# Two weight buffers for the block products, and an output projection in halves of 512 columns

## The chip, the cores and the metric

The kernel runs on one core of a Trainium2 chip. The metric is the device time of one execution in microseconds (us), here the median of 3 runs. A profiled execution gives the trace from which all rows below come; its engines are called PE (matrix multiplication, with its weight loads as PEld), DVE (vector), ACT (scalar activations), POOL, and SP, which here only issues DMA transfers.

## The reference

One layer on x of 1024 tokens by 1024 features, in float32. What matters here:

```
h = rmsnorm(x, g_mix)
u, c_g, b_g, q, k, v, sg, m_c, m_r = split(h @ w_in)         # nine blocks of columns
y_conv = (b_g * causal_dwconv(c_g * u, conv_w)) @ w_out_conv   # 3 taps along the tokens
o = rmsnorm(retention(rope(q), rope(k), v), g_ret)
y_ret = (silu(sg) * o) @ w_out_ret
x = x + (sigmoid(m_c) * y_conv + sigmoid(m_r) * y_ret) @ w_o   # the output projection
x = x + hier_moe(rmsnorm(x, g_moe), ...)                       # 32 experts, 2 per token
ple = rmsnorm(p @ w_ple_proj, g_ple_post)
x = x + sigmoid(rmsnorm(x, g_ple_in) @ w_ple_gate) * ple
out = rmsnorm(x, g_final)
```

## The kernel before

Every float32 product is made of three fp32r products (mm3, lines 192 to 195): the operands are split into a high part, which ACT writes (split, L188), and a low part, which DVE writes (L189), and PE adds high by high, high by low and low by high.

The products with w_in for u, c, b, sg, m_c and m_r go in blocks of 256 columns. One block (seven, L409 on) loads 1 MB of weights into a part of the buffer `both` (L411), forms sums of its quarters on DVE (L441 into `bt`, L442 in place in `both`, L443 into `bt`), splits seven pieces `pc`, and PE runs seven partial products of 12 matmuls of 128x512 each, with the token halves in the rotating accumulators sa, sb, sc, sd. Between them ACT (L452) and DVE (L453, L457, L458, and L464 to L467) combine the accumulators; the fourth product into sd may start only when L458 has read sd. The list of blocks has 24 entries: n = 0 to 7 (m_c, m_r) together with the retention, which uses `both[:, 1]` for its chunks; n = 8 to 19 are u, c and b for four groups of columns (conv_pair); n = 20 to 23 are sg. `raw()` gives the place of the block's weights: always `both[:, 0]`. In conv_pair DVE also makes the three taps (L490 to L492) and L497.

After that the mix (y, out_conv and out_ret) and the output projection (out_proj, L558) run for each half of 512 tokens, hf = 0 and 1. out_proj goes by quarters of 256 columns of w_o: 512 KB chunks of weights (`wor`, L199; split into `wos`), two accumulators `oa` and `ob` that hold two token tiles each, then DVE adds x (in `ring`, loaded by L566) and multiplies by the gain of the expert norm; PE turns the result (h2q, h2p, L595), ACT or DVE copies it (h2T), and PE multiplies by the router's weights (lp, L604). x2d and h2d are stores for later stages. In hf = 1 `look(i)` (L734) issues the first expert loads `raw`. Then come the router (lg), the projection of p (ple: pa, stores to pled, L796) and the experts (L908 to L953).

The tiles are allocated from pools and a scheduler fixes the order of each engine's instructions before the run; every engine executes its own list in order. SP has at most eight DMAs outstanding: each issue also waits for the one eight before it.

Of the kernel before, what the change touches and what calls it, by code (L numbers as in the profile page):

```python
# [10 lines left out]
F32 = mybir.dt.float32  # L11
F32R = mybir.dt.float32r
BF = mybir.dt.bfloat16
I32 = mybir.dt.int32
AF = mybir.ActivationFunctionType
OP = mybir.AluOpType
# [4 lines left out]
S, D, NH, DK, DV = 1024, 1024, 8, 64, 128  # L21
# [54 lines left out]
def tile_kernel(ctx, tc, cst, x, p, g_mix, w_in, conv_w, g_ret, w_out_conv, w_out_ret, w_o, g_moe,  # L76
                w_rg, b_rg, w_re, b_re, w_exp_gate, w_exp_up, w_exp_down, g_ple_in, w_ple_gate,
                w_ple_proj, g_ple_post, g_final, out, dbg=None, stop=99):
    nc = tc.nc
    V, A, P, T, Y = nc.vector, nc.scalar, nc.gpsimd, nc.tensor, nc.sync  # L80
    dbg = dbg or {}
    x, p, out = x[0], p[0, 0], out[0]
    w_in, w_o, w_out_conv, w_out_ret = w_in[0], w_o[0], w_out_conv[0], w_out_ret[0]
# [15 lines left out]
    wk = dst.enter_context(tc.tile_pool(name="wk", bufs=2, side="right", reuse_waits="tile"))  # L99
    ps = dst.enter_context(tc.tile_pool(name="ps", bufs=1, space=PSUM, reuse_waits="tile"))  # L100

    def bt(name, dt=F32R):
        return big.tile([128, 4096], dt, name=name, tag="big", bufs=8)

    def w2k(name, dt=F32):
        return wk.tile([128, 512], dt, name=name, tag="w2k", bufs=NW)

    def row2(name, src):
        g = [w2k(name), w2k(name)]
        for i in range(2):  # L110
            Y.dma_start(out=g[i], in_=bass.AP(tensor=src.tensor, offset=src.offset + i * 512, ap=[[0, 128], [1, 512]]))
        return g

    def acc(name):
        return ps.tile([128, 512], F32, name=name, tag="acc", bufs=4)

    def trp(name):
        return ps.tile([128, 4, 128], F32, name=name, tag="tr", bufs=1)
# [6 lines left out]
    wr = xgb[:, 644:1412].rearrange("p (k n) -> p k n", k=8)  # L125
# [20 lines left out]
    ident = cs[:, C_ID:C_ID + 128]  # L146
# [30 lines left out]
    x2d = dram.tile([S, D], F32, name="x2d")  # L177
    h2d = dram.tile([S, D + 1], F32, name="h2d")
# [8 lines left out]
    def split(src, hi, lo):  # L187
        a = A.activation(hi, src, AF.Copy)  # L188
        V.tensor_tensor(lo, src, hi, op=OP.subtract)  # L189
        return a.ins  # L190

    def mm3(o, lh, ll, rh, rl, start, stop, skip=False):
        T.matmul(o, lh, rh, start=start, stop=False, skip_group_check=skip)  # L193
        T.matmul(o, lh, rl, start=False, stop=False, skip_group_check=skip)  # L194
        return T.matmul(o, ll, rh, start=False, stop=stop, skip_group_check=skip).ins  # L195

    def wraw(src, k0, nk, c0, nn, name):
        raw = rawp.tile([128, 1024], F32, name=name + "r", tag="raw", bufs=2)
        Y.dma_start(out=raw.rearrange("p (k n) -> p k n", k=nk),  # L199
                    in_=src[k0 * 128:(k0 + nk) * 128, c0:c0 + nn].rearrange("(k p) n -> p k n", p=128))  # L200
        return raw

    def wchunk(src, k0, nk, c0, nn, name):
        raw = ahead.pop() if ahead else wraw(src, k0, nk, c0, nn, name)
        hl = wp.tile([128, 2, 1024], F32R, name=name + "s", tag="hl", bufs=3)
        with tc.issue_after(started.pop()) if started else nullcontext():
            split(raw, hl[:, 0], hl[:, 1])
        return hl.rearrange("p s (k n) -> p s k n", k=nk)
# [319 lines left out]
    def parts(src, hf, at=None):  # L528
        hi, lo = (bt(n).rearrange("p (f t) -> p f t", f=8) for n in ("ph", "pl"))
        for f in range(0, 8, 2) if at else ():  # L530
            split(at[f // 4][:, f % 4:f % 4 + 2], hi[:, f:f + 2], lo[:, f:f + 2])
        for f in range(8) if not at else ():
            t = w2k("pr")
            Y.dma_start(out=t, in_=src[f * 128:f * 128 + 128, hf * 512:hf * 512 + 512])
            split(t, hi[:, f], lo[:, f])
        return hi, lo
# [19 lines left out]
                then()  # L556

    def out_proj(hf, mhv, mlv, gm):  # L558
        ring = bt("ring", F32).rearrange("p (r t n) -> p r t n", r=4, t=4)
        ss = wk.tile([128, 4, 4], F32, name="x2ss", bufs=2)  # L560
        lp = ps.tile([128, 4, 128], F32, name="lp", tag="kv", bufs=1)
        h2l = shared.rearrange("p (t n) -> p t n", t=4)
        rows = slice(hf * 512, hf * 512 + 512)

        def load(cc):
            Y.dma_start(out=ring[:, cc % 2],  # L566
                        in_=x[rows, cc * 256:cc * 256 + 256].rearrange("(t p) n -> p t n", p=128))

        load(0)
        for cc in range(4):  # L570
            a = [acc("oa"), acc("ob")]
            ck = slice(cc * 256, (cc + 1) * 256)
            x2 = ring[:, cc % 2]
            h2 = ring[:, 2 + cc % 2] if cc < 3 else h2l[:, :, 0:256]
            if cc < 3:
                load(cc + 1)
            for kh in range(2):
                wc = wchunk(w_o, kh * 4, 4, cc * 256, 256, "wo")
                for t in range(4):
                    for k in range(4):  # L580
                        kk = kh * 4 + k
                        mm3(a[t // 2][:, (t % 2) * 256:(t % 2) * 256 + 256],
                            mhv[:, kk, t * 128:(t + 1) * 128], mlv[:, kk, t * 128:(t + 1) * 128],
                            wc[:, 0, k], wc[:, 1, k], kk == 0 and t % 2 == 0, kk == 7, True)
            for b in range(2):
                tt = slice(2 * b, 2 * b + 2)
                V.tensor_tensor(x2[:, tt], a[b].rearrange("p (t n) -> p t n", t=2), x2[:, tt], op=OP.add)
                V.tensor_tensor(h2[:, tt], x2[:, tt], gm[cc // 2][:, None, (cc % 2) * 256:(cc % 2) * 256 + 256].to_broadcast([128, 2, 256]), op=OP.mult)
                for t in (2 * b, 2 * b + 1):
                    j = w2k("x2j", BF)[:, 0:256]  # L590
                    A.activation(j, x2[:, t], AF.Square, accum_out=ss[:, t, cc:cc + 1])
                pt = trp("h2p") if b else ps.tile([128, 4, 128], F32, name="h2q", tag="S", bufs=1)
                for t in (2 * b, 2 * b + 1):
                    for j in range(2):
                        T.transpose(pt[:, (t % 2) * 2 + j], h2[:, t, j * 128:(j + 1) * 128], ident)  # L595
                hT = w2k("h2T").rearrange("p (a b) -> p a b", a=4)
                if b == 0:
                    A.activation(hT, pt, AF.Copy)
                else:
                    V.tensor_copy(hT, pt)  # L600
                for t in (2 * b, 2 * b + 1):
                    for j in range(2):
                        k = 2 * cc + j
                        T.matmul(lp[:, t, 0:96], hT[:, (t % 2) * 2 + j], wr[:, k],  # L604
                                 start=cc == 0 and t == 0 and j == 0, stop=k == 7, skip_group_check=True)
            Y.dma_start(out=x2d[rows, ck].rearrange("(t p) n -> p t n", p=128), in_=x2)
            if cc < 3:
                Y.dma_start(out=h2d[rows, ck].rearrange("(t p) n -> p t n", p=128), in_=h2)
            if hf == 1 and cc < 2:
                look(cc)  # L610
        return ss, lp, h2l


# [103 lines left out]
    def wview(e, w):  # L717
        src, k = wsrc[w]
        return src[e].rearrange("(p k) n -> p (k n)", k=k)
# [7 lines left out]
    def look(i):  # L727
        for c in order[len(raws):i + 1]:
            raws[c] = bt("raw", F32)
            for h in range(2):  # L730
                late = len(raws) == 8 and h == 1
                sl = slice(h * 2048, h * 2048 + 2048)
                with tc.issue_after(gathers[-1]) if late else nullcontext():
                    (P if late else Y).dma_start(out=raws[c][:, sl], in_=wview(*c)[:, sl])  # L734
# [79 lines left out]
            'S3': (*s34, 0), 'S4': (*s34, 4)}  # L814
    both = bt("both", F32).rearrange("p (r n) -> p r n", r=2)

    def raw():
        return both[:, 0]

    for n in range(8):  # L820
        gate_pair(n // 4, n % 4, raw, left, retention(n, both[:, 1]))
# [15 lines left out]
    z, r = parts(zd, 0, zr), parts(rd, 0)  # L837
    for hf in range(2):
        mhv, mlv = (bt(n).rearrange("p (f t) -> p f t", f=8) for n in ("mh", "ml"))
        mix(hf, z, r, mhv, mlv, (lambda: router(0, *late)) if hf else None)  # L840
        if hf == 0:
            r, z = parts(rd, 1), parts(zd, 1)
        gm = row2("gm", g_moe)
# [403 lines left out]
```

## Time and profile before

| what | value |
|---|---|
| median of 3 runs | 1788.19 us (1787.86 to 1793.71) |
| the profiled execution | 1788.15 us, of which the trace's span is 1786.4 us |
| PE busy | 1720.2 us, 96% of the span |
| DVE, ACT, POOL busy | 1269.6, 903.3, 157.6 us |
| mean granted PE clock | 0.989 |
| moved by DMA | 397.68 MB, mean 223 GB/s |

Times of the trace count from the span's start. "Busy" of PE is modelled: matmuls overlap in the pipeline, so the duration of one is longer than the distance from one start to the next. "Idle before" of a row is the time in which its engine had nothing to run, and the releaser is what ended it.

### The profile page before, as it was taken

How to read it: one execution, taken by the hardware profiler on the slowest of the kernel's cores; microseconds unless marked ns; L12 is line 12 of the kernel's file. 1: busy time of each engine (PE TensorE's matmuls, PEld its weight loads, DVE VectorE, ACT ScalarE, POOL GpSimd, SP SyncE). 2: the span in 40 equal slices, each digit the busy share in tenths (PEclk: the TensorE clock that was granted, in tenths of full speed). 3: DMA queues.
4: the chain of work that ended last, by engine and by line, in shares of the span. 5: the costliest groups of instructions: out<-in, count | busy, mean ns of one | idle time of the engine just before them, and what ended most of it. 6: DMA issues, size and time to landing. Idle time of an engine off the chain costs nothing. (4 is left out here: it accounts for less than half of the span.)

```text
span 1786.4 us, 22831 instructions
## 1 busy us (share of the span) xinstructions
PE 1720.2 (96%) x8447; PEld 1348.9 (76%) x8447; DVE 1269.6 (71%) x1747; ACT 903.3 (51%) x1354; POOL 157.6 (9%) x157
## 2 busy tenths in 40 slices
PE   6999999999999999899999998999999999999697
PEld 5878788888787878788988975676767676666586
DVE  5559576675776776646464467999999988888674
ACT  4343443443222223424322347888888877778542
POOL 1000000000000000000000013121212221100010
PEclk9999999999999999999999999999999999999899
DMA  6534444433113226657666879999999999996561
GB/s 226 155 103 136 153 133 144 137 119 106 63 56 118 71 94 190 189 185 227 166 194 200 272 231 356 365 369 382 378 372 374 369 373 351 368 397 267 202 253 64
DMA packets 174628, 397.68 MB, mean 223 GB/s; under 512 B 14796, under 2 KB 101908, under 8 KB 148916
## 3 DMA queue, kind: packets, MB, share of 16 engines
q1 hardware_dynamic: 165012, 378.19, 61.0%
q0 software_dynamic: 9504, 18.02, 3.3%
q8 instruction: 67, 1.10, 0.3%
q14 instruction: 45, 0.37, 0.1%
HBM read 344.77 MB, written 57.68 MB: 225 GB/s over the span
## 5 line engine op out<-in xcount | busy, mean ns | idle before, releaser
L910 DVE TENSOR_TENSOR hc<-raw,hc 128x1024 fp32r<-128x1024 f32 x128 | 154.3, 1223 | 21.1 <-ACT hc L908 20.0
L910 DVE TENSOR_TENSOR hb<-raw,hb 128x1024 fp32r<-128x1024 f32 x128 | 153.9, 1220 | 15.2 <-ACT hb L908 13.8
L910 DVE TENSOR_TENSOR ha<-raw,ha 128x1024 fp32r<-128x1024 f32 x128 | 154.1, 1222 | 13.7 <-ACT ha L908 11.7
L908 ACT ACTIVATE ha<-raw 128x1024 fp32r<-128x1024 f32 x128 | 132.7, 1058 | 26.6 <-PE y L195 15.3
L908 ACT ACTIVATE hb<-raw 128x1024 fp32r<-128x1024 f32 x128 | 132.8, 1057 | 21.1 <-PE u L195 11.6
L908 ACT ACTIVATE hc<-raw 128x1024 fp32r<-128x1024 f32 x128 | 132.6, 1057 | 17.2 <-PE y L195 5.1
L188 ACT ACTIVATE pc<-both 128x512 fp32r<-128x512 f32 x120 | 73.0, 625 | 120.9 <-PE sc L195 53.0
L193 PE MATMUL y<-ph,wys 128*128 128x512 f32 x256 | 101.5, 397 | 3.3 <-ACT wys L188 3.3
L195 PE MATMUL y<-ph,wys 128*128 128x512 f32 x256 | 101.1, 395 | 0.9 <-DVE wys L189 0.9
L194 PE MATMUL y<-pl,wys 128*128 128x512 f32 x256 | 100.8, 394 | 0.0
L189 DVE TENSOR_TENSOR pc<-both,pc 128x512 fp32r<-128x512 f32 x120 | 81.2, 688 | 16.5 <-ACT pc L188 16.2
L188 ACT ACTIVATE wys<-wyr 128x1024 fp32r<-128x1024 f32 x32 | 34.0, 1061 | 98.9 <-PE y L195 71.8
L193 PE MATMUL sd<-sh,pc 128*128 128x512 f32 x192 | 76.3, 398 | 3.9 <-DVE u L458 3.9
L188 ACT ACTIVATE pc<-bt 128x512 fp32r<-128x512 f32 x48 | 30.0, 626 | 91.3 <-DVE bt L443 90.9
L195 PE MATMUL sd<-sh,pc 128*128 128x512 f32 x192 | 74.9, 390 | 0.0
L194 PE MATMUL sd<-sl,pc 128*128 128x512 f32 x192 | 74.9, 390 | 0.0
L189 DVE TENSOR_TENSOR wqs<-wqr,wqs 128x1024 fp32r<-128x1024 f32 x32 | 39.2, 1225 | 49.4 <-ACT wqs L188 49.2
L188 ACT ACTIVATE wqs<-wqr 128x1024 fp32r<-128x1024 f32 x32 | 33.9, 1059 | 70.2 <-PE qa L195 62.3
L452 ACT ACTIVATE u<-sa 128x512 f32<-128x512 f32 x24 | 14.4, 598 | 98.6 <-PE sa L195 59.0
L757 POOL DMA_INDIRECT xgb<-h2d,ii x32 | 35.5, 1110 | 300.1 <-DVE hd L946 198.6
L545 DVE TENSOR_TENSOR msg<-y,msg 128x512 f32<-128x512 f32 x32 | 22.1, 690 | 53.8 <-PE y L195 53.6
L193 PEld LDWEIGHTS y<-ph,wys 128*128 128x128 f32 x256 | 48.7, 190 | 14.0 <-ACT wys L188 4.2
(393 smaller groups left out, 4980.2 us busy)
## 6 DMA issues: line engine op xcount, KB each, us to landing
raw<-in_w_exp_gate_dram SPq DMA_DIRECT2D x64, 1024.0 KB, 20.4
raw<-in_w_exp_up_dram SPq DMA_DIRECT2D x64, 1024.0 KB, 19.3
raw<-in_w_exp_down_dram SPq DMA_DIRECT2D x63, 1024.0 KB, 20.4
both<-in_w_in_dram SPq DMA_DIRECT2D x24, 1024.0 KB, 5.9
wqr<-in_w_in_dram SPq DMA_DIRECT2D x32, 512.0 KB, 3.8
qd<-r SPq DMA_DIRECT2D x32, 256.0 KB, 2.4
both<-qd SPq DMA_DIRECT2D x8, 1024.0 KB, 4.9
wyr<-in_w_out_conv_dram SPq DMA_DIRECT2D x16, 512.0 KB, 4.4
```

Of the source, the lines that this page charges most:

```text
L188: a = A.activation(hi, src, AF.Copy)
L189: V.tensor_tensor(lo, src, hi, op=OP.subtract)
L193: T.matmul(o, lh, rh, start=start, stop=False, skip_group_check=skip)
L194: T.matmul(o, lh, rl, start=False, stop=False, skip_group_check=skip)
L195: return T.matmul(o, ll, rh, start=False, stop=stop, skip_group_check=skip).ins
L452: A.activation(u2, a, AF.Copy)
L545: V.tensor_tensor(sg, y, sg, op=OP.mult)
L757: g = P.indirect_dma_start(out=xgs[e % 3], out_offset=None, in_=h2d, in_offset=bass.IndirectOffsetOnAxis(ap=ii[:, 0, e:e + 1], axis=0), bo ...
L908: A.activation(hl[:, 0, q:q + 1024], raw[:, q:q + 1024], AF.Copy)
L910: V.tensor_tensor(hl[:, 1, q:q + 1024], raw[:, q:q + 1024], hl[:, 0, q:q + 1024], op=OP.subtract)
```

## The change

The first part: from block n = 8 to n = 19 the weights go to `both[:, 0]` and `both[:, 1]` in turn. The second part: out_proj goes by two halves of 512 columns. A chunk of w_o is then two rows of 128 by 512 columns (512 KB as before), each token tile has an accumulator of its own (four at once), a matmul has 512 columns, the two x loads of 1 MB both stand ahead of the weights, and the products for the router are taken tile by tile. The normed rows h2 go to the buffers h2a and h2b of the tag w2k, from which also h2T and x2j are allocated, and are stored in pieces of 256 KB. `look` moves inside the loop over chunks.

```diff
     def out_proj(hf, mhv, mlv, gm):
-        ring = bt("ring", F32).rearrange("p (r t n) -> p r t n", r=4, t=4)
+        ring = bt("ring", F32).rearrange("p (r t n) -> p r t n", r=2, t=4)
...
-        load(0)
-        for cc in range(4):
-            a = [acc("oa"), acc("ob")]
...
-            if cc < 3:
-                load(cc + 1)
-            for kh in range(2):
-                wc = wchunk(w_o, kh * 4, 4, cc * 256, 256, "wo")
+        for cc in range(2):
+            Y.dma_start(out=ring[:, cc], in_=x[rows, cc * 512:cc * 512 + 512].rearrange("(t p) n -> p t n", p=128))
+        for cc in range(2):
+            a = [acc("oa") for _ in range(4)]
+            x2 = ring[:, cc]
+            for kc in range(4):
+                wc = wchunk(w_o, kc * 2, 2, cc * 512, 512, "wo")
                 for t in range(4):
...
+                        mm3(a[t], mhv[:, kk, t * 128:(t + 1) * 128], mlv[:, kk, t * 128:(t + 1) * 128],
+                            wc[:, 0, k], wc[:, 1, k], kk == 0, kk == 7)
+                if hf == 1 and kc == 3 - 2 * cc:
+                    look(cc)
             for b in range(2):
                 tt = slice(2 * b, 2 * b + 2)
...
+                h2 = [w2k("h2a").rearrange("p (t n) -> p t n", t=2),
+                      h2l[:, tt, 0:256] if cc else w2k("h2b").rearrange("p (t n) -> p t n", t=2)]
                 for t in (2 * b, 2 * b + 1):
...
+                    pt = trp("h2p") if t % 2 else ps.tile([128, 4, 128], F32, name="h2q", tag="S", bufs=1)
+                    for j in range(4):
+                        T.transpose(pt[:, j], h2[j // 2][:, t % 2, (j % 2) * 128:(j % 2) * 128 + 128], ident)
...
     def raw():
-        return both[:, 0]
+        taken.append(0)
+        n = len(taken) - 1
+        return both[:, n % 2 if 8 <= n < 20 else 0]
```

The order on DVE changes in the convolution. These are its instructions around the combination u3_3965 of block n = 12 (bt_4057 belongs to n = 13, bt_4189 to n = 14; pc are low halves of pieces), first before:

```order
498 L453 TENSOR_TENSOR u2_3964<-sb_3916,u2_3964 128x512
499 L441 TENSOR_TENSOR bt_4057<-both_1562 128x512
500 L442 TENSOR_TENSOR both_1562<-both_1562 128x4x128
501 L443 TENSOR_TENSOR bt_4057<-both_1562 128x512
502 L457 TENSOR_TENSOR u3_3965<-sc_3917,u2_3964 128x512
503 L189 TENSOR_TENSOR pc_4065<-bt_4057,pc_4065 128x512
504 L458 TENSOR_TENSOR u3_3965<-sd_3918,u3_3965 128x512
```

and in the changed kernel:

```order
501 L189 TENSOR_TENSOR pc_4065<-bt_4057,pc_4065 128x512
502 L453 TENSOR_TENSOR u2_3964<-sb_3916,u2_3964 128x512
503 L189 TENSOR_TENSOR pc_4080<-both_1562,pc_4080 128x512
504 L441 TENSOR_TENSOR bt_4189<-both_1562 128x512
505 L442 TENSOR_TENSOR both_1562<-both_1562 128x4x128
506 L457 TENSOR_TENSOR u3_3965<-sc_3917,u2_3964 128x512
507 L189 TENSOR_TENSOR pc_4095<-both_1562,pc_4095 128x512
508 L458 TENSOR_TENSOR u3_3965<-sd_3918,u3_3965 128x512
509 L443 TENSOR_TENSOR bt_4189<-both_1562 128x512
```

Between L453 and L458 stood all three sums of the next block; now two of the sums of the block after that stand there, with a split ahead of them, and the next block's own sums were made one block earlier.

PE at the end of the first group of columns of out_proj in hf = 0, where the accumulators oa_6401 or oa_6446 begin the next group. Before:

```order
3428 L195 MATMUL ob_6257<-wos_6314,ml_5627 128x256
3429 L595 MATMUL h2q_6371<-cs_75,ring_6252 128x128 x4
3430 L193 MATMUL oa_6401<-wos_6406,mh_5626 128x256
...
3439 L193 MATMUL oa_6401<-wos_6406,mh_5626 128x256
3440 L604 MATMUL lp_6254<-xgb_76,h2T_6376 128x96 x4
3441 L595 MATMUL h2p_6388<-cs_75,ring_6252 128x128 x4
```

In the changed kernel:

```order
3430 L593 MATMUL h2q_6385<-cs_75,h2b_6378 128x128 x2
...
3432 L593 MATMUL h2p_6398<-cs_75,h2b_6378 128x128 x2
3433 L193 MATMUL oa_6446<-wos_6452,mh_5626 128x512
3434 L194 MATMUL oa_6446<-wos_6452,mh_5626 128x512
3435 L195 MATMUL oa_6446<-wos_6452,ml_5627 128x512
3436 L601 MATMUL lp_6254<-xgb_76,h2T_6390 128x96 x4
3437 L193 MATMUL oa_6446<-wos_6452,mh_5626 128x512
...
3440 L193 MATMUL oa_6447<-wos_6452,mh_5626 128x512
3441 L601 MATMUL lp_6254<-xgb_76,h2T_6403 128x96 x4
```

Both transposed tiles now come first, and three wide matmuls stand between them and the first lp where ten narrow ones stood.

SP at the start of out_proj in hf = 1, first before:

```order
316 L566 DMA ring_7491<-in_x_dram 128x4x256 x2
317 L199 DMA wor_7498<-in_w_o_dram 128x4x256
318 L199 DMA wor_7551<-in_w_o_dram 128x4x256
319 L734 DMA raw_7640<-in_w_exp_gate_dram 128x2048 x2
320 L199 DMA wor_7646<-in_w_o_dram 128x4x256
```

then in the changed kernel:

```order
316 L565 DMA ring_7288<-in_x_dram 128x4x512 x2
317 L199 DMA wor_7297<-in_w_o_dram 128x2x512
318 L199 DMA wor_7326<-in_w_o_dram 128x2x512
319 L731 DMA raw_7413<-in_w_exp_gate_dram 128x2048
320 L199 DMA wor_7355<-in_w_o_dram 128x2x512
```

The two loads of x that stand ahead of the first chunk of w_o have twice the bytes; half of the first expert load now follows the fourth chunk.

## Rows read from the trace of the kernel before

**Rows 1.** Busy time of each engine in windows, with granted clock, DMA share, GB/s.

```profile
430.00:720.00 290.00, 282.38 (x1233) 230.12 (x1232) 203.00 (x322) 75.08 (x131) 4.48 (x8) 1.00 0.31 98
837.00:900.00 63.00, 62.79 (x503) 60.67 (x502) 28.90 (x45) 20.42 (x48) 1.01 (x1) 1.00 0.63 183
...
970.00:985.00 15.00, 14.52 (x68) 11.95 (x67) 7.69 (x10) 3.81 (x4) 0.00 (x0) 1.00 1.00 351
...
1100.00:1700.00 600.00, 585.63 (x2718) 404.58 (x2717) 528.03 (x553) 472.69 (x587) 103.40 (x91) 0.99 0.95 351
```

**Rows 2.** Waits from 430 to 720 us: total, times, longest.

```profile
DVE bt L441 <- DMA both<-in_w_in_dram: 19.7, 14, 2.8
...
PE sd L193 <- DVE u L458: 3.9, 5, 1.4
PE sb L193 <- ACT pc L188: 3.7, 4, 1.0
```

**Rows 3.** Timeline, start of block n = 11: start, duration, idle before.

```profile
478.31 0.37 SPq L411 DMA_DIRECT2D both<-in_w_in_dram  x1
...
484.01 0.69 DVE L441 TENSOR_TENSOR bt<-both 128x512 f32<-128x512 f32 x1 [2.66 <-DMA both<-in_w_in_dram]
...
486.94 0.50 PE L193 MATMUL sb<-sh,pc 128*128 128x512 f32 x1 [0.87 <-ACT pc L188]
```

**Rows 4.** Timeline inside block n = 12.

```profile
516.26 0.69 DVE L441 TENSOR_TENSOR bt<-both 128x512 f32<-128x512 f32 x1 [0.38 <-DMA both<-in_w_in_dram]
...
519.77 0.69 DVE L458 TENSOR_TENSOR u<-sd,u 128x512 f32<-128x512 f32 x1
...
520.51 0.50 PE L193 MATMUL sd<-sh,pc 128*128 128x512 f32 x1 [0.55 <-DVE u L458]
```

**Rows 5.** Timeline of PE, first quarter of out_proj in hf = 0.

```profile
837.19 0.28 PE L193 MATMUL oa<-wos,mh 128*128 128x256 f32 x1
...
848.70 0.60 PE L595 MATMUL h2q<-cs,ring 128*128 128x128 f32 x4
...
850.59 1.10 PE L604 MATMUL lp<-xgb,h2T 128*128 128x96 f32 x8
```

**Rows 6.** Chain of waits into out_proj of hf = 1: start, duration, what.

```profile
964.93 0.23 PE y L195
...
972.41 0.24 PE y L195
...
973.47 8.16 DMA wor<-in_w_o_dram
981.74 1.07 ACT wos L188
982.83 1.24 DVE wos L189
```

**Rows 7.** Timeline of PE, the start of out_proj in hf = 1.

```profile
984.11 0.39 PE L194 MATMUL oa<-wos,mh 128*128 128x256 f32 x1 [0.48 <-DVE wos L189]
```

**Rows 8.** Windows at the start of the mix, columns as in Rows 1.

```profile
742.00:745.60 3.60, 1.85 (x7) 1.24 (x8) 3.57 (x6) 3.60 (x6) 0.00 (x0) 0.99 0.03 12
745.60:748.90 3.30, 3.30 (x9) 2.54 (x8) 3.30 (x6) 1.37 (x3) 0.00 (x0) 0.50 0.93 312
```

**Rows 9.** Timeline from the end of out_proj in hf = 1 to the first expert.

```profile
1039.13 0.60 PE L595 MATMUL h2q<-cs,shared 128*128 128x128 f32 x4
...
1046.19 0.80 PE L193 MATMUL pa<-wpl,pp 128*128 128x512 f32 x1 [1.24 <-ACT pp L188]
...
1075.74 0.69 DVE L795 TENSOR_TENSOR po<-pa,pin 128x512 f32<-128x512 f32 x1 [0.75 <-DMA pled<-po]
...
1078.87 0.73 PE L193 MATMUL g<-hc,xh 128*88 128x512 f32 x1 [5.15 <-ACT xh L188]
```

**Rows 10.** DMA issues of the whole run: count, KB each, median us to landing.

```profile
zd<-cv SPq DMA_DIRECT2D x16, 256.0 KB, 3.3
...
h2d<-ring SPq DMA_DIRECT2D x6, 512.0 KB, 6.3
```

More of the change, by code (lines that the diff above doesn't have):

```diff
@@ L558, in out_proj @@
     def out_proj(hf, mhv, mlv, gm):
-        ring = bt("ring", F32).rearrange("p (r t n) -> p r t n", r=4, t=4)
-        ss = wk.tile([128, 4, 4], F32, name="x2ss", bufs=2)
+        ring = bt("ring", F32).rearrange("p (r t n) -> p r t n", r=2, t=4)
+        ss = wk.tile([128, 4, 2], F32, name="x2ss", bufs=2)
         lp = ps.tile([128, 4, 128], F32, name="lp", tag="kv", bufs=1)
@@ L563, in out_proj @@
         rows = slice(hf * 512, hf * 512 + 512)
-        def load(cc):
-            Y.dma_start(out=ring[:, cc % 2],
-                        in_=x[rows, cc * 256:cc * 256 + 256].rearrange("(t p) n -> p t n", p=128))
-        load(0)
-        for cc in range(4):
-            a = [acc("oa"), acc("ob")]
-            ck = slice(cc * 256, (cc + 1) * 256)
-            x2 = ring[:, cc % 2]
-            h2 = ring[:, 2 + cc % 2] if cc < 3 else h2l[:, :, 0:256]
-            if cc < 3:
-                load(cc + 1)
-            for kh in range(2):
-                wc = wchunk(w_o, kh * 4, 4, cc * 256, 256, "wo")
-                for t in range(4):
[L580 to L584, printed above, removed]
+        for cc in range(2):
+            Y.dma_start(out=ring[:, cc], in_=x[rows, cc * 512:cc * 512 + 512].rearrange("(t p) n -> p t n", p=128))
@@ new lines, in out_proj @@
+        for cc in range(2):
[3 more added lines that the diff above has]
+                wc = wchunk(w_o, kc * 2, 2, cc * 512, 512, "wo")
+                for t in range(4):
+                    for k in range(2):
+                        kk = kc * 2 + k
+                        mm3(a[t], mhv[:, kk, t * 128:(t + 1) * 128], mlv[:, kk, t * 128:(t + 1) * 128],
+                            wc[:, 0, k], wc[:, 1, k], kk == 0, kk == 7)
+                if hf == 1 and kc == 3 - 2 * cc:
+                    look(cc)
@@ L585, in out_proj @@
             for b in range(2):
                 tt = slice(2 * b, 2 * b + 2)
-                V.tensor_tensor(x2[:, tt], a[b].rearrange("p (t n) -> p t n", t=2), x2[:, tt], op=OP.add)
-                V.tensor_tensor(h2[:, tt], x2[:, tt], gm[cc // 2][:, None, (cc % 2) * 256:(cc % 2) * 256 + 256].to_broadcast([128, 2, 256]), op=OP.mult)
+                h2 = [w2k("h2a").rearrange("p (t n) -> p t n", t=2),
+                      h2l[:, tt, 0:256] if cc else w2k("h2b").rearrange("p (t n) -> p t n", t=2)]
@@ L589, in out_proj @@
                 for t in (2 * b, 2 * b + 1):
-                    j = w2k("x2j", BF)[:, 0:256]
-                    A.activation(j, x2[:, t], AF.Square, accum_out=ss[:, t, cc:cc + 1])
[L592 to L610, printed above, removed]
+                    V.tensor_tensor(x2[:, t], a[t], x2[:, t], op=OP.add)
+                for c in range(2):
+                    V.tensor_tensor(h2[c], x2[:, tt, c * 256:c * 256 + 256],
+                                    gm[cc][:, None, c * 256:c * 256 + 256].to_broadcast([128, 2, 256]), op=OP.mult)
+                for t in (2 * b, 2 * b + 1):
+                    j = w2k("x2j", BF)[:, 0:512]
+                    A.activation(j, x2[:, t], AF.Square, accum_out=ss[:, t, cc:cc + 1])
+                    pt = trp("h2p") if t % 2 else ps.tile([128, 4, 128], F32, name="h2q", tag="S", bufs=1)
+                    for j in range(4):
+                        T.transpose(pt[:, j], h2[j // 2][:, t % 2, (j % 2) * 128:(j % 2) * 128 + 128], ident)
+                    hT = w2k("h2T").rearrange("p (a b) -> p a b", a=4)
+                    if t % 2 == 0:
+                        A.activation(hT, pt, AF.Copy)
+                    else:
+                        V.tensor_copy(hT, pt)
+                    for j in range(4):
+                        k = 4 * cc + j
+                        T.matmul(lp[:, t, 0:96], hT[:, j], wr[:, k], start=cc == 0 and t == 0 and j == 0,
+                                 stop=k == 7, skip_group_check=True)
@@ L611, in out_proj @@
+                r0 = hf * 512 + 256 * b
+                for c in range(2 - cc):
+                    c0 = cc * 512 + c * 256
+                    Y.dma_start(out=h2d[r0:r0 + 256, c0:c0 + 256].rearrange("(t p) n -> p t n", p=128), in_=h2[c])
+            Y.dma_start(out=x2d[rows, cc * 512:cc * 512 + 512].rearrange("(t p) n -> p t n", p=128), in_=x2)
         return ss, lp, h2l
@@ L815, in tile_kernel @@
     both = bt("both", F32).rearrange("p (r n) -> p r n", r=2)
+    taken = []
     def raw():
-        return both[:, 0]
+        taken.append(0)
+        n = len(taken) - 1
+        return both[:, n % 2 if 8 <= n < 20 else 0]
     for n in range(8):
```

## The prediction

> **What bounds the kernel now.** I read the windows first. In the two long stretches PE has almost no time to give: 282.38 of 290 us in the blocks of u, c, b and sg, and 585.63 of 600 us among the experts [rows 1]. DVE is busy 203.00 of the 290 us, so the convolution is bound by PE and by the few places where PE waits for DVE or ACT. The list of waits names them: PE waits 3.9 us at the fourth product into sd for L458, in 5 places, and 3.7 us at the first product sb of a block for a piece from ACT, in 4 places [rows 2]. With 290 - 282.38 = 7.6 us idle, these two are all of it. In out_proj I read the start distances, the timeline around its beginning in hf = 1, and the chain of waits.
>
> **The blocks of u, c, b.** The wait for sb stands where a u follows a b. The load for n = 11 is issued at 478.31, DVE gets it at 484.01, then makes the sums, and PE starts at 486.94 after 0.87 us idle [rows 3]. That load can be issued only when the block before has given up the same half of `both`. With the halves in turn, the u has its data and its sums a block earlier, about 19 us (84 matmuls of 0.227 us, worked out below); a lateness of 0.9 us goes. The 3.7 us of the four places go.
>
> The wait for sd has another form. In n = 12 DVE takes up the sums of the next block before L457: L441 waits for the DMA till 516.26, L458 starts at 519.77, and PE is freed at 520.51, 0.55 us late [rows 4]. The changed order keeps a load at nearly this place: the half of `both` is free when the last piece is split, as before, so the load that L441 awaits (now for the block after the next) lands at the same time. But one sum less stands ahead of L458, and a split more stands ahead of L441, where DVE waited for the DMA anyway. The sum costs 0.69 us [rows 4], so L458 comes about 0.7 us earlier, less some 0.3 us where the split does not fit into the wait of 0.38 us: 0.55 us late becomes about 0.1 early. Of the 3.9 us, 0.6 us belong to sg, which the change does not touch; of the other 3.3 us I leave 0.6 for places where a load comes later than this. In the b blocks L458 gets a split ahead of it, and I count nothing, since no such place is among the rows of waits; at worst it brings 0.5 us (one split beyond what slack there is) in each of four blocks.
>
> Sum: -3.7 - 2.7 = -6.4 us. Bounds: -3.7 if the order only keeps the waits for sd, -7.0 if all go; with the b blocks at their worst -1.7.
>
> **The matmuls of out_proj.** A narrow one takes (848.70 - 837.19) / 96 = 0.120 us from start to start [rows 5]; a wide one, measured on y, (972.41 - 964.93) / 33 = 0.2267 us [rows 6]. Per half of the tokens 384 narrow ones (46.1 us) become 192 wide ones (43.5 us): -2.55 us, twice. Transposes and router products keep their number.
>
> The Trainium skill, "TensorE: Matmul & The Clock Gate", section "Back-to-back issue gap", gives N/2.4 + 2.5 ns from one matmul to the next at the full clock. By that 384 fewer matmuls save only 384 x 2.5 ns, some 1.0 us instead of 5.1 (an estimate from that page). The two distances of the rows above are both this kernel's own, with its weight loads, and 0.240 against 0.2267 us differ by 13 ns, so the rows decide.
>
> **Ends of the groups of columns, hf = 0.** Before, ten narrow matmuls (1.2 us) stood between the transposes and the first router product; after, three wide ones (0.7 us) and four more transposes. ACT must copy h2T in this time, and in its list a split of w_o stands ahead, whose buffer comes free with the last matmul of the old group: 1.07 us like [rows 6] and a copy of 0.6, against 0.7 + 0.7 us of cover: 0.3 us idle. At the end of the half the same again. So hf = 0 nets -2.55 + 0.6 = -2.0 us. There is a wait here that the trace of before does not show: h2T is in the same pool as h2a and h2b, and so two of its copies wait until a store of h2 has landed. Such a store is issued when the sums of its two tiles are done, about 1 us before the group's last matmul ends, and the copy is due after two tiles of transposes (0.60 us each, [rows 5]), two of router products (1.10 each, [rows 5]) and seven wide matmuls (1.6), which overlap: some 5.5 us from issue to use. Stores of 256 KB take 3.3 us (zd), those of h2 with 512 KB 6.3 us [rows 10]. I take the smaller, which has the size, so nothing; the upper bound is 0.8 us and, behind other loads, more: that is a rival.
>
> **Start of out_proj, hf = 1.** Here PE waits already: the first chunk is issued at 973.47 and takes 8.16 us behind two loads of x of 0.5 MB each, then 1.07 us on ACT and 1.24 on DVE [rows 6], and PE is idle 0.48 us at 984.11 [rows 7]. Now 1 MB more stands ahead of it. The windows say that the transfers are the bound there: DMA share 1.00 at 351 GB/s from 970 to 985 [rows 1], so 1 MB is 3.0 us. (Bounds: none, if the first two chunks overtake the x load; 3.0 + 0.5.) PE's list offers four products of the high part first (0.9 us) where it had two narrow ones, so of 3.0 us about 2.2 to 2.6 would show; I take 2.0 us more idle, 2.5 in all, since x and chunk share the engines.
>
> Does the clock fall after this? The windows at the start of the mix show the price: from 742 to 745.6 PE is busy for only 1.85 of 3.6 us, and then the granted clock is 0.50 (1.2 GHz) from 745.6 to 748.9 [rows 8], which costs half of 3.3 us, 1.6 us. A wait of 0.87 us in the convolution costs none: the clock is 1.00 from 430 to 720 [rows 1]. There PE was idle for 1.75 us, and 2.5 us is beyond that, so I count 1.6 us. Beside it: the Trainium skill, same page, section "HAM oscillation", says that waits for a DMA between bursts of matmuls send the engine to the low clock; the rows above agree in direction.
>
> So hf = 1 is -2.55 + 2.0 + 1.6 = +1.05 us, with 0.3 for the end of its first group: +1.35.
>
> **From the end of out_proj to the experts.** The last matmul's end at 1039.13 is followed by pa at 1046.19 and the last po at 1075.74 [rows 9]. In the changed order the squares x2j of the last tile and the transposes of four tiles come later, by about three instructions of ACT, 0.6 us each: pa starts some 1.8 us later. But the last po waits for stores of pled (0.75 us before it alone), and PE stands 5.15 us before g [rows 9]. With pa later, its stores are spread and this wait shrinks. I set this stage at 0, with bounds of -1 (fewer stores outstanding) and +2 (pa's delay passed on in full).
>
> **Experts.** Their order is the same, and PE is the bound; the gain before them is kept. DMA share 0.95 there [rows 1] leaves it a risk: if the loads were the bound, an earlier start would be lost.
>
> **Sum.** -6.4 - 2.0 + 1.35 + 0 = -7.05 us. The profiled execution took 1788.15 us, 0.04 from the median; so 1781.1 us. Adding the bounds that are independent: the convolution between -7.0 and -1.7, hf = 1 between -2.3 (no delay, no clock) and +3, the stage behind it -1 to +2.
>
> **Rivals.**
> 1. Stall at out_proj is gone or halved: the first chunk does not suffer from the x loads, and the clock stays up. Then 1781.1 - 3.6 = 1777.5 us. For it: at 351 GB/s 8.16 us would move 2.9 MB, while x and the chunk are 1.5 MB, so other loads that are in flight take part of the time, and less so later. Against it: the share of 1.00, and that those loads are the same after the change.
> 2. The sd waits stay, and the b blocks take their own: -1.7 to -3.7 instead of -6.4, thus 1784 to 1786, within 0.3% of before. For it: L441 still awaits a DMA ahead of L457, and what lands later than 5.7 us (484.01 - 478.31) is on the path again.
> 3. **Slower:** the stores of h2 hold the copies h2T. Each of the four ends of a group has two of these copies. A store that lands d us after its issue stalls PE by d - 5.5 us; at an end with loads of w_o and of the experts on the queue (8.16 us for 0.5 MB in [rows 6]) that is 2.7 us, and with the low clock 1.6 more. At four ends 4 x 4.3 = 17 us, thus some 1798; from d = 7.3 us on at all four ends (4 x 1.8 = 7.1) the kernel is no longer faster. Against it: in hf = 0 the DMA share is only 0.63 at 183 GB/s from 837 to 900 [rows 1].
> 4. Experts bound by DMA: the gain before them vanishes, about 1787. Against it: PE is busy 98% of the time.
>
> **How the numbers follow.** A measurement of this kernel tells about 0.3%, 5.4 us, from no change: faster is below 1782.8 and slower above 1793.6. The forecast, 1779.5 to 1782.7 with its small terms, gets 0.42; rival 1 0.15; rival 2 0.22; rival 3 0.15, of which 0.09 above 1793.6; rival 4 0.06. The forecast's own spread puts 0.04 of its 0.42 above 1782.8, and partial cases of rival 2 put 0.04 below it. So faster 0.38 + 0.15 + 0.04 = 0.57; slower 0.09; the rest, 0.34, is the same. The range of 8 in 10 runs from 1777 to 1789: it holds the forecast, rivals 2 and 4, most of rival 1 and the lighter part of rival 3.
>
> **What would show it.** The waits of PE for ACT pc at sb are gone between 430 and 720, and PE is busy above 282 us in a stretch some 6 us shorter; waits for L458 below 1.3 us. Wide oa matmuls at 0.227 us. In hf = 1 a wait of PE for wos of about 2.5 us, followed by a stretch at 0.50. No wait of ACT or DVE at h2T on a store of h2d. The last po about 37 us behind the end of the last oa. Wrong it would be, above all, by loads that land later in the convolution, or by stores of h2 that take 8 us.

## The result and the profile after

The changed kernel takes 1780.94 us (median of 6 runs, 1778.87 to 1782.91), the kernel before on the same chip 1789.05 us (1787.86 to 1793.71): a ratio of 0.995, 95% interval 0.9939 to 0.9961. The prediction was 1781.1 us, faster. The profiled execution takes 1780.42 us with a span of 1778.6 us, 7.8 us less than before.

Where did the 7.8 us come from? The first instruction of some stages stands in both timelines, and the distances between them are the stages:

| stage (from first to first) | before | after | difference |
|---|---|---|---|
| start to the first product of n = 8 | 426.02 | 425.16 | -0.86 |
| n = 8 to the mix (first y) | 316.97 | 311.60 | -5.37 |
| mix of hf = 0 (y to oa) | 94.20 | 93.12 | -1.08 |
| out_proj hf = 0 and mix hf = 1 | 146.17 | 145.19 | -0.98 |
| out_proj hf = 1 to the first pa | 62.83 | 61.62 | -1.21 |
| pa to the first g | 32.68 | 33.72 | +1.04 |
| g to the end | 707.53 | 708.19 | +0.66 |

The change does not touch the stages of the first, the third and the last row; together they give 1.28 of the 7.8 us. In the fourteen traces of this study the third lies between 92.9 and 96.1 us, and the last between 707.1 and 711.2, whatever was edited elsewhere; so a difference of 1 us there says nothing.

The waits from 425 to 715 us in the changed kernel, to be held against [rows 2] (total, times, longest):

```profile
DVE bt L441 <- DMA both<-in_w_in_dram: 9.1, 10, 1.6
...
PE sd L193 <- DVE u L458: 3.5, 5, 1.2
```

The wait at sb for ACT is gone. That at sd for L458 has kept its size, but not its places: before it stood in n = 8, 9, 12 and 18, now in n = 8, 11, 14, 17 and 20 (and one of sg before, at 717 us, is gone). The timeline in n = 11, the block of [rows 3], shows how:

```profile
486.69 0.69 DVE L497 TENSOR_TENSOR cv<-u,cv 128x512 f32<-128x512 f32 x1
487.29 0.69 DVE L189 TENSOR_TENSOR pc<-both,pc 128x512 fp32r<-128x512 f32 x1
...
488.01 0.38 SPq L411 DMA_DIRECT2D both<-in_w_in_dram  x1
...
494.58 0.69 DVE L441 TENSOR_TENSOR bt<-both 128x512 f32<-128x512 f32 x1 [1.38 <-DMA both<-in_w_in_dram]
...
495.92 0.68 DVE L457 TENSOR_TENSOR u<-sc,u 128x512 f32<-128x512 f32 x1
...
497.12 0.69 DVE L458 TENSOR_TENSOR u<-sd,u 128x512 f32<-128x512 f32 x1
...
497.86 0.50 PE L193 MATMUL sd<-sh,pc 128*128 128x512 f32 x1 [1.17 <-DVE u L458]
498.19 0.40 PE L194 MATMUL sd<-sl,pc 128*128 128x512 f32 x1
```

The load for n = 13 is issued at 488.01 and lands 6.6 us later, where that of [rows 3] took 5.7. L441 waits for it in DVE's list, ahead of L457 and L458, and PE waits 1.17 us for L458. The load is also issued late: it follows the split of the last piece (the L189 at 487.29), which stands behind L497 in DVE's list. Without its wait PE would have gone on at 496.69, 8.68 us after this issue; in n = 12 of the kernel before, by the rows of [rows 4] and an issue at 510.55, it was 9.41 us. The two PE rows also show that a wait costs more than its idle time. From one start to the next there are 0.33 us here, 0.10 above the 0.2267 of [rows 6], and the matmul before counts as busy for 0.39 us, 0.16 longer than it holds up the next. So each wait costs its idle time and about 0.27 us. The length of whole blocks agrees: n = 11 takes 20.51 us from its first product to that of n = 12, and 19.04 in run e5 below, where the wait is gone. Before, nine waits had 7.57 us idle, thus 10.0 us lost; after, five have 3.50, thus 4.85: the difference of 5.15 is nearly the 5.37 of the table.

PE in out_proj of hf = 0, the first wide matmul and the first transposes, answering to [rows 5]:

```profile
829.88 0.39 PE L193 MATMUL oa<-wos,mh 128*128 128x512 f32 x1
...
851.65 0.38 PE L593 MATMUL h2q<-cs,h2a 128*128 128x128 f32 x2
...
853.54 0.32 PE L601 MATMUL lp<-xgb,h2T 128*128 128x96 f32 x1 [0.15 <-issue]
```

96 wide matmuls take 21.77 us, 0.2268 us each, and the lp that was to wait 0.3 us waits 0.15. In hf = 1 there are two waits, at the start and at the end of the first group of columns; first the start, answering to [rows 7], and two windows around it (columns as in [rows 1]):

```profile
975.07 0.50 PE L193 MATMUL oa<-wos,mh 128*128 128x512 f32 x1 [1.60 <-ACT wos L188]
```

```profile
973.00:976.50 3.50, 1.83 (x8) 0.89 (x7) 2.83 (x4) 2.54 (x3) 0.00 (x0) 1.00 0.77 320
976.50:981.00 4.50, 4.50 (x21) 3.69 (x22) 1.51 (x2) 0.76 (x2) 0.00 (x0) 1.00 0.46 154
```

The granted clock stays at 1.00 (2.4 GHz) through the wait and behind it. The mix of hf = 0, the same program in both kernels, shows a pair that is closer still. There y waits for its weights wys, 2.17 us before and 2.29 us after the change. These are the 4 us up to the end of that wait and the 4 us behind it, first before:

```profile
755.00:759.00 4.00, 1.83 (x9) 1.17 (x7) 1.49 (x4) 1.06 (x1) 0.00 (x0) 1.00 1.11 324
759.00:763.00 4.00, 3.82 (x9) 2.60 (x10) 2.44 (x2) 1.06 (x1) 0.00 (x0) 0.57 0.93 294
```

then in the changed kernel:

```profile
748.80:752.80 4.00, 1.71 (x9) 1.10 (x7) 1.73 (x4) 1.06 (x1) 0.00 (x0) 1.00 1.08 313
752.80:756.80 4.00, 3.47 (x14) 2.57 (x15) 2.41 (x2) 1.06 (x1) 0.00 (x0) 1.00 0.95 305
```

The clock fell before the change and not after it. The second wait of out_proj in hf = 1, in the timeline of SP, ACT and PE:

```profile
990.68 4.12 SPq L199 DMA_DIRECT2D wor<-in_w_o_dram  x2
...
1000.73 1.06 ACT L188 ACTIVATE wos<-wor 128x1024 fp32r<-128x1024 f32 x1 [4.98 <-DMA wor<-in_w_o_dram]
1001.69 0.58 ACT L596 ACTIVATE h2T<-h2q 128x512 f32<-128x512 f32 x1
...
1002.33 0.35 PE L601 MATMUL lp<-xgb,h2T 128*128 128x96 f32 x1 [3.27 <-ACT h2T L596]
```

The split that stands ahead of h2T in ACT's list waits 4.98 us for its chunk of w_o, and PE 3.27 us for the copy behind it. The chunk itself is needed only two chunks of matmuls later.

The rows from the end of out_proj to the first expert, answering to [rows 9]:

```profile
1036.69 0.51 PE L193 MATMUL pa<-wpl,pp 128*128 128x512 f32 x1 [1.24 <-ACT pp L188]
...
1066.56 0.60 ACT L790 ACTIVATE pj<-pa 128x512 bf16<-128x512 f32 x1 [3.04 <-DMA pled<-po]
...
1070.41 0.73 PE L193 MATMUL g<-hc,xh 128*88 128x512 f32 x1 [5.43 <-ACT xh L188]
```

The last piece of the projection of p waits for a store of pled to give its buffer back, as po did before.

### The profile page after: what moved, and what is told of

Same layout as the page of the kernel before. It is cut to its first block, busy times and chain, and to the rows that moved or that the text cites. A ratio compares the mean times of both kernels' runs of the same rounds, so it can differ in the third digit from the quotient of the medians.

```text
span 1778.6 us, 22039 instructions
## 1 busy us (share of the span) xinstructions
PE 1712.2 (96%) x8063; PEld 1327.4 (75%) x8063; DVE 1266.2 (71%) x1747; ACT 903.2 (51%) x1322; POOL 158.2 (9%) x157
## 3 DMA queue, kind: packets, MB, share of 16 engines
q8 instruction: 64, 1.05, 0.2%
## 4 chain that ended last, share of the span: by engine, by line
PE 74%; issue 14%; DMA 6%; DVE 4%; ACT 1%; POOL 0%; SPq 0%; POOLq 0%; DVEq 0%; ACTq 0%
PE y L195 4%; PE y L193 4%; PE y L194 4%; PE qa L194 3%; PE qa L193 3%; PE g L193 3%; PE qa L195 3%; PE g L194 3%; PE g L195 3%; PE u L194 3%; PE u L193 3%; PE u L195 3%; DMA both<-in_w_in_dram 3%; PE sd L193 2%; PE sc L193 2%
## 5 line engine op out<-in xcount | busy, mean ns | idle before, releaser
L189 DVE TENSOR_TENSOR pc<-both,pc 128x512 fp32r<-128x512 f32 x120 | 82.2, 688 | 26.4 <-ACT pc L188 26.0
L189 DVE TENSOR_TENSOR wqs<-wqr,wqs 128x1024 fp32r<-128x1024 f32 x32 | 39.2, 1226 | 49.2 <-ACT wqs L188 49.2
L193 PEld LDWEIGHTS y<-ph,wys 128*128 128x128 f32 x256 | 48.5, 189 | 13.9 <-ACT wys L188 4.3
L195 PEld LDWEIGHTS y<-ph,wys 128*128 128x128 f32 x256 | 48.4, 189 | 12.2 <-DVE wys L189 2.2
```

## The experiments

My theory after this: the buffers bring 5.4 us, out_proj 2.7 us in hf = 0 and nothing in hf = 1, where two waits and the stage behind it take the gain. Rivals: out_proj brings nearly all; the blocks only trade waits; the width of a matmul matters little. The stages of all runs, in us, as in the table above (hf = 0 with the mix of hf = 1). Each ratio below is to the kernel before, run beside it, with its 95% interval. The ratios of e4 to e8, 0.994 to 0.9953, are not clear of the changed kernel's 0.995 (0.9939 to 0.9961), so what these runs show is read from their stages and waits, in one trace each:

| run | n = 8 to y | y to oa | hf = 0 | hf = 1 to pa | pa to g | g to end |
|---|---|---|---|---|---|---|
| before | 316.97 | 94.20 | 146.17 | 62.83 | 32.68 | 707.53 |
| after | 311.60 | 93.12 | 145.19 | 61.62 | 33.72 | 708.19 |
| e1_buffers | 310.74 | 94.36 | 146.15 | 62.48 | 31.62 | 708.81 |
| e2_proj | 318.60 | 92.88 | 145.17 | 58.65 | 34.56 | 708.77 |
| e3_narrow | 311.30 | 93.68 | 148.22 | 61.37 | 34.53 | 708.26 |
| e4_copyfirst | 311.29 | 95.23 | 145.09 | 59.44 | 33.87 | 708.60 |
| e5_sumsbehind | 307.45 | 93.55 | 145.31 | 61.06 | 32.59 | 707.35 |
| e6_xlater | 310.76 | 94.14 | 143.41 | 58.04 | 35.01 | 707.09 |
| e7_looklater | 312.15 | 94.28 | 145.08 | 59.30 | 34.83 | 707.21 |
| e8_fewerslots | 310.90 | 96.04 | 145.68 | 58.69 | 29.74 | 709.97 |
| e9_both | 307.07 | 94.90 | 143.42 | 58.03 | 34.48 | 709.52 |
| e10_three | 307.91 | 92.89 | 143.39 | 58.03 | 31.21 | 708.44 |
| e11_oldproj | 306.50 | 96.07 | 146.16 | 62.68 | 31.12 | 711.19 |
| e12_before_slots | 317.92 | 93.99 | 146.16 | 62.74 | 30.58 | 709.88 |

**e1, the buffers alone** (the kernel before, with the new `raw()`).

> Only the first part of the change: the two halves of the weight buffer in turn, out_proj as before. My theory: the waits of PE at the first product of a block (3.7 us) go, those at L458 are moved and not removed, and a wait also costs about 0.1 us of restart, so the kernel is 5.4 us faster than before, about 1783.6 us. Rival: the gain is out_proj's, and the blocks only trade one wait for another; then it is at most 2 us faster, 1787 or more.

1783.78 us against 1790.13 before, ratio 0.9962 (0.9949 to 0.9975). The stretch of the blocks is 6.2 us shorter. Its waits of PE from 425 to 725 us:

```profile
PE sd L193 <- DVE u L458: 2.9, 5, 0.8
```

There is none at sb. The rival that the blocks only trade one wait for another falls, though in part it is right: the waits at sd are as many as before.

**e2, out_proj alone** (the changed kernel, `raw()` always returning `both[:, 0]`).

> Only the second part: out_proj by halves of 512 columns, one weight buffer as before. My theory: hf = 0 gains 2.7 us, hf = 1 nothing or loses up to 1.5 us because PE waits for the first chunk of w_o and for the copy h2T, so 1.5 to 2.5 us faster than before, about 1787 us. Rival: out_proj brings most of the gain, 5 us or more, 1784 or less.

1791.64 against 1790.13 us, ratio 1.0 (0.9989 to 1.0012): no gain in the measured time. The stages show why the trace is kinder: hf = 0 is 1.0 us shorter and hf = 1 4.2, since the wait at lp is only 0.31 us in this run, but pa to g and what follows take 1.9 and 1.2 back, and the blocks, which are those of before, took 1.6 longer by themselves. Both expectations missed; that the gain does not get past the first expert is a part I had put too low. The profiled execution took 1787.82 us, 3.8 less than the median, so this trace is not a typical one. The intervals of e1 (0.9962) and of the changed kernel (0.995) overlap too: that the second part adds anything in the changed kernel is not shown by measured times, only by its stages.

**e3, the price of a width.**

```diff
+                    for c in range(2):
+                        cs2 = slice(c * 256, c * 256 + 256)
...
+                            mm3(a[t][:, cs2], ..., wc[:, 0, k, cs2], wc[:, 1, k, cs2], kk == 0 and c == 0, kk == 7, True)
```

> The changed kernel, but each product of out_proj with 512 columns is issued as two of 256 columns, everything else as it is. By the start distances of the trace before (0.120 and 0.2267 us) it is 5.1 us slower than the changed kernel, about 1786 us, less what the waits in hf = 1 hide. Rival, by a fixed cost of 2.5 ns for each matmul: 1.0 us slower, about 1782 us. The start distance of the narrow matmuls in the trace decides directly.

1786.07 us, ratio to the kernel before 0.9974 (0.9963 to 0.9985), against 0.995 for the changed kernel: 0.0024, or 4.3 us, where 5.1 were expected. The first group of columns in its timeline:

```profile
831.32 0.28 PE L193 MATMUL oa<-wos,mh 128*128 128x256 f32 x1
...
854.35 0.38 PE L595 MATMUL h2q<-cs,h2a 128*128 128x128 f32 x2
```

192 narrow matmuls take 23.03 us, 0.1199 each, against 21.77 for 96 wide ones: 1.26 us in a group, 2.5 us in a half, where the lists are otherwise the same. The gain is the width's.

**e4, the copy ahead of the split** (the split of the third chunk of the second group is issued after the first h2T).

> The changed kernel, but ACT copies h2T of the first tile before it splits the third chunk of w_o of the second group of columns, in both halves. My theory: the wait of 3.27 us at lp in hf = 1 comes only from ACT's order, so it goes, and PE does not wait for this chunk later: about 3 us faster than the changed kernel, 1778 us. Rival: the late load of the chunk is the cause, and the wait moves to the oa that need it: no gain.

1780.74 us, ratio 0.994 (0.9927 to 0.9954). The wait of 3.27 us is gone, the chunk is not waited for later, and hf = 1 is 2.2 us shorter, but another wait shows behind it:

```profile
1004.13 0.60 ACT L599 ACTIVATE h2T<-h2q 128x512 f32<-128x512 f32 x1 [1.58 <-DMA h2d<-h2a]
1004.78 0.41 PEld L604 LDWEIGHTS lp<-xgb,h2T 128*128 128x128 f32 x3 [1.41 <-ACT h2T L599]
1004.78 0.46 PE L604 MATMUL lp<-xgb,h2T 128*128 128x96 f32 x2 [0.97 <-ACT h2T L599]
```

Here the copy waits for the store of h2a, the wait that was the third rival of the prediction: it exists, at one of the four ends, and costs 0.97 us. The test is weaker than it looks: in e2, e3 and e8, where ACT's order is that of the changed kernel, the wait for the split was 0.31, 0 and 0.33 us. It comes and goes with the landing of the chunk. In the measured time the expected 3 us do not show.

**e5, the sums behind L458.**

```diff
+        with tc.issue_after(summeds[-2]) if 10 <= len(summeds) <= 20 else nullcontext():
+            V.tensor_tensor(t3, b22, b12, op=OP.subtract)
```

> The changed kernel, but in the blocks of u, c, b and the first of sg the sums of the block after the next (L441 to L443) stand behind L458 in DVE's list. My theory: the waits at the fourth product into sd that are left (3.5 us in five places) come from L441, which waits for its load ahead of L457 and L458; they go, the stretch from the first of these blocks to the mix gets 3 to 4 us shorter, and the kernel takes about 1777.5 us. Rival: DVE is simply late after the taps; then the waits stay or move to the first product of a block, and nothing is gained.

1777.6 us, ratio 0.994 (0.9924 to 0.9957). One wait is left from 425 to 740 us:

```profile
PE sd L193 <- DVE u L461: 0.7, 1, 0.7
```

The stretch is 4.15 us shorter than in the changed kernel. The place of these sums in DVE's list, with L441's wait for its load, was the cause; the run moves the wait and the sums together and does not part the two. The rival falls as it was put, since the waits are gone; that DVE is late there (L497 ahead of the last split, above) still delays the load that L441 awaits.

**e6, the loads of x later** (behind the first and the third chunk of w_o, in both halves).

> The changed kernel, but the two loads of x in out_proj stand behind the first and the third chunk of w_o. My theory: the first chunk is no longer behind 2 MB, and PE's wait of 1.60 us at the start of out_proj in hf = 1 goes. Whether the kernel gets 1.5 us faster depends on what follows: if the stage up to the first expert is bound by its transfers or stores, the first g starts no earlier, and the time is the same.

1777.9 us, ratio 0.994 (0.9927 to 0.9952). The first matmuls of hf = 1 no longer wait, and the first chunk is now split long before them:

```profile
961.16 0.38 SPq L199 DMA_DIRECT2D wor<-in_w_o_dram  x1
962.65 0.38 SPq L566 DMA_DIRECT2D ring<-in_x_dram  x1
966.73 1.07 ACT L188 ACTIVATE wos<-wor 128x1024 fp32r<-128x1024 f32 x1 [0.32 <-DMA wor<-in_w_o_dram]
...
973.56 0.39 PE L193 MATMUL oa<-wos,mh 128*128 128x512 f32 x1
```

With no load of x ahead of it, the chunk reaches ACT 5.6 us after its issue, against 8.2 in [rows 6]. The later chunks come in time too, so hf = 1 is 3.6 us shorter, of which pa to g takes 1.3 back.

**e7, the second expert load two chunks later** (`look(1)` at kc == 3).

> The changed kernel, but the second expert load of out_proj in hf = 1 is issued two chunks later. My theory: the 2 MB of this load ahead of the third chunk made ACT late, so the wait of 3.27 us at lp goes and pa starts 3 us earlier, but the first g comes at most 1 us earlier, since the stores of the projection of p hold it: within 1.5 us of the changed kernel. Rival: the 3 us arrive at the end, 1778 us or less.

1780.39 us, ratio 0.9946 (0.9933 to 0.9959). hf = 1 is 2.3 us shorter; 1.1 of it is lost before g. That is near what was expected, and within the noise of the changed kernel. Here too an h2T waits for the store of h2a, and PE for it 0.71 us.

**e8, fewer buffers in the projection of p.**

```diff
-                j = w2k("pj", BF)[:, 0:512]
-                A.activation(j, a, AF.Square, accum_out=ss[:, t, b:b + 1])
                 o = w2k("po")
+                A.activation(o, a, AF.Square, accum_out=ss[:, t, b:b + 1])
```

> The changed kernel, but in the projection of p the squares of a tile go into the buffer of its product, so that two buffers of the tag w2k are taken for each piece and not three, and a store has longer to land. If the buffers hold the first expert (my theory), the wait of 3.04 us of ACT pj for a store goes and the first g comes 2 to 3 us earlier after the last pa: about 1778.5 us. Rival: the transfers themselves bound this stage (DMA share 1.0); then g waits for something else and the time stays.

1780.16 us, ratio 0.9953 (0.9939 to 0.9968). The wait of pj for the store goes, and pa to g is 4.0 us shorter. Of these, 2.35 lie behind the last pa, as expected. The other 1.6 lie among the pa and are the clock's; the 4 us in question in the changed kernel and in this run:

```profile
1038.00:1042.00 4.00, 3.89 (x12) 3.10 (x13) 3.09 (x17) 1.51 (x5) 0.00 (x0) 0.57 0.95 252
```

```profile
1040.00:1044.00 4.00, 3.91 (x19) 3.15 (x20) 3.86 (x22) 2.24 (x7) 0.00 (x0) 1.00 1.01 251
```

But g to the end is 1.8 longer: the first product with xl, three matmuls behind the first g, waits 1.86 us for xl, whose split waits for a store of pled. So the rival is right in this run.

**e9 and e10, the edits together.**

> The changed kernel with two of the edits tried before: the sums behind L458, and the loads of x behind the first and third chunk. If the two gains lie in stages that don't meet (my theory), they add: the stretch of the blocks about 307.4 us, no wait at the first oa of hf = 1, and 6 to 8 us faster than the changed kernel, about 1774 us. Rival: the earlier start of the experts is lost to their transfers; then it is no faster than the better of the two alone, 1777.5 us.

> The same with the squares in the buffers of the products in the projection of p. If what held the first g was only the buffers, it comes 2 us earlier and the kernel takes 1772 us; if the transfers bound this stage (my theory now), g comes earlier and the next waits behind it take it back: within 1 us of the kernel with the two edits.

e9 takes 1776.09 us, ratio 0.9917 (0.9904 to 0.9931), e10 1770.54 us (1770.08 to 1771.58), ratio 0.9891 (0.9876 to 0.9907). In e9 the gains of the two stages add: 307.07 for the blocks as in e5, 143.42 and 58.03 in out_proj as in e6. e10 missed its expectation on the good side: 5.5 us less than e9, where I expected 1 at most. pa to g is 3.3 us shorter there and 1.1 less is spent behind g; the other 2.0 stand in the mix, which the edit does not touch: there y waits 4.63 us for wys in e9, and 1.96 and 0.53 us in e10. In e9 the first product with xl waits 1.69 us, in e10 1.05 us:

```profile
1059.86 0.47 PE L193 MATMUL g<-hc,xh 128*88 128x512 f32 x1 [3.09 <-ACT xh L188]
1061.32 0.95 DVE L189 TENSOR_TENSOR xl<-xp,xh 128x352 fp32r<-128x352 f32 x2 [0.41 <-issue]
...
1061.90 0.73 PE L195 MATMUL g<-hc,xl 128*88 128x512 f32 x1 [1.05 <-DVE xl L189]
```

**e11, e10 with the old out_proj.**

> The kernel with three edits, but with out_proj as it was before the change: quarters of 256 columns, two accumulators. My theory: out_proj by halves is worth its 2.5 us in hf = 0 and, since nothing stalls it now, 2 us more in hf = 1, so this is 4 to 5 us slower than the kernel with three edits, about 1775 us. Rival, after the run of the second part alone: out_proj by halves is worth nothing, and this takes the same 1770 to 1771 us.

1782.18 us, ratio 0.9951 (0.9937 to 0.9964): 0.0060 or some 11 us slower than e10, more than either expectation. Of it 2.8 us lie in hf = 0 and 4.65 in hf = 1; 3.2 lie in the mix before, which is the same code, and 2.75 behind g, where PE waits 4.04 us for xl. So out_proj by halves, with the loads of x behind the first chunk, is worth about 7.4 us where nothing stalls it.

**e12, the kernel before with fewer buffers.**

> The kernel before, with only the squares of the projection of p in the buffers of the products. If the stores of p held the first expert there too (DVE waits for them in three places, 3.9 us in all), g comes about 2.5 us earlier after the last pa and the kernel takes 1787 us or less. Rival: the transfers bound this stage, g or the next waits behind it stay, and the time is that of before.

1791.43 us, ratio 1.0009 (1.0 to 1.0018): no gain, the rival. g comes 2.1 us earlier after pa, and then:

```profile
1079.82 0.73 PE L193 MATMUL g<-hc,xh 128*88 128x512 f32 x1 [3.03 <-ACT xh L188]
...
1083.04 0.95 DVE L189 TENSOR_TENSOR xl<-xp,xh 128x352 fp32r<-128x352 f32 x2 [2.18 <-DMA pled<-po]
...
1083.62 0.73 PE L195 MATMUL g<-hc,xl 128*88 128x512 f32 x1 [2.22 <-DVE xl L189]
```

The wait for the stores of pled has only moved from po to xl.

## Why the prediction was right

The time came out within 0.2 us of the median, and the mechanism and its sign were right. That it came out so close is luck. The forecast was 7.05 us less than before; the medians lie 8.1 apart. In the trace the touched stages give 6.5 of the 7.8 us, and of their terms several were off and made up for each other.

**Blocks: -6.4 predicted, -5.4 in the trace, -6.2 in e1.** The waits at sb went, as stated. The step on the sd waits failed: they were to come down to some 1.2 us with sg's, and 3.5 us stayed. The prediction held that the load is issued and lands at the same point as before. In n = 11, 14 and 17 it was issued some 0.7 us later than in n = 12 before, measured against the moment when PE needs L458, and it took 5.9 to 6.6 us instead of 5.7; so L441 stood on the path again. The second half of this is the condition that rival 2 named. The extra waits in the b blocks, which it named too, did not come. The size came out nearly right since each of the four waits fewer also saves its 0.27 us, which the prediction left out. e5 shows the cause.

**Width: -2.55 for each half predicted.** e3 measures 2.5 in hf = 0: two narrow matmuls take 0.240 us from start to start where a wide one takes 0.2267. The Trainium skill ("TensorE: Matmul & The Clock Gate", section "Back-to-back issue gap") gives a gap of N/2.4 + 2.5 ns for isolated matmuls, and says that it does not hold for a stream with a weight load for each; by it a half would have gained 0.5 us (an estimate from that page). The two traces do not agree with that figure for these matmuls, each with its own weight load.

**hf = 0: -2.0 predicted.** PE waited 0.15 us at the ends of the groups where 0.6 was counted, so the term was too small. The table's -0.98 holds also the start of hf = 1, where PE waits 1.60 us more; in e6, where that wait is gone, the stage is 2.76 us shorter than before.

**Start of hf = 1: 2.5 us idle predicted, 1.60 measured**; e6 shows that the 2 MB ahead were the cause. **Clock: +1.6 predicted, 0 measured.** This step failed. The stretch is idle for 1.67 of 3.5 us, that of [rows 8] for 1.75 of 3.6, and only the second is followed by 0.50. The two waits of y in the mix (2.17 and 2.29 us) part in the same way, and in e3 and e8 PE waits 2.18 and 2.10 us at this start and the clock stays at 1.00. Idle time of this size does not tell whether the clock falls. The Trainium skill's section "HAM oscillation" on the same page expects a drop from waits for a DMA that are long enough; the trace shows none here.

**In its place** came the wait of 3.27 us at lp, which the prediction did not have at this size: it had seen the split ahead of h2T, but took it to wait for a buffer and not for a load. It is not in every run (0 to 3.3 us).

Rival 1 was in good part what happened: the clock stayed up, and the wait at the start grew by 1.1 us where 2.0 was counted. But its reason, that the loads of x do not hold the first chunk, is wrong: e6 shows that they do.

**End of out_proj.** pa was to start 1.8 us later for the order at the end. From the end of the last oa (ob before) to the first pa there are 8.36 us, where there were 6.90: 1.46 later, near that size. But it is no loss. Transposes and router products that stood ahead of the last oa now stand in this stretch and fill it: ahead of pa's own wait PE is idle for 0.25, 0.25 and 0.27 us, where it was 1.17, 0.78 and 0.18 before. The prediction counted the work that comes later and not the idle time that it fills. With these 1.4 us and the width, hf = 1 is worth over 4 us when the wait at lp is short or gone (e2; e10 against e11).

**Up to the first expert: 0 predicted (-1 to +2), +1.04 measured from pa to g**, or +2.5 from the end of the last oa, where the prediction starts to count; of that the 1.46 are the moved work. Rival 3, the stores of h2, shows in e4 and e7 with 0.7 to 1.0 us at one end, far from what was needed to turn the sign. (In its sum, 4 x 1.8 is 7.2 and not 7.1; nothing hangs on it.) Rival 4 fell: what was gained ahead of the experts, as in e5 and e10, arrives at the end.

Open is in part why the edit of e8 pays in e10 and not in e12. In e9, to which e10 compares, the first product with xl waits 1.69 us already, and 1.05 in e10; in the changed kernel and in the one before it does not wait, and with the edit it waits 1.86 us (e8) and 2.22 us (e12). So in these two the edit trades one wait for another. The traces of e8, e11 (4.04 us) and e12 name stores of pled for it, those of e9 and e10 no DMA; what sets when they land was not taken apart. Of e10's lead over e9, the 2.0 us in the mix are y's wait for wys and not the edit's.

## What to carry to other kernels

A second buffer takes away the wait for its load only if what awaits the next load does not stand ahead of urgent work in an in-order list; look where the first reader of a buffer stands on its engine, not only when the load is issued. Price a new width by start distances in the same kernel, and add to each wait of TensorE what its restart costs. When a gain disappears a stage later, go from first instruction to first instruction and look which wait has taken its place before calling the stage bound by transfers.

## What the runs showed of the hardware that was not expected

Each wait of PE among 128x512 matmuls cost about 0.27 us beyond the idle time that the profile lists. A stretch with 1.67 of 3.5 us idle left the granted clock at 1.00, another with 1.75 of 3.6 was followed by 0.50. In the mix of hf = 0, the same program in both kernels, a wait of 2.17 us was followed by 4 us at a mean of 0.57, and one of 2.29 us by 1.00. That mix took between 92.9 and 96.1 us in the fourteen traces: y waits between 1.95 and 4.63 us for wys at one place, and the stretches of low clock differ (in e8 0.54 from 754 to 761.5 us).
